# A plain down product for one group in the first token block, its weight sums made a block later

## The chip, the cores and the metric

The kernel runs on one core of one Trainium2 chip. Its engines are TensorE (PE, whose weight loads the profile lists as PEld), VectorE (DVE), ScalarE (ACT), GpSimd (POOL) and SyncE (SP), which issues all of the kernel's DMAs. The metric is the device time of one execution in microseconds, as the median of several runs.

## The reference

The reference is one inference step of a hybrid encoder layer on 2048 prompt tokens and 32 sample tokens, in 32-bit floats: a mixer, then a feed-forward, then a last norm. The part that this case touches is the feed-forward:

```python
h = rmsnorm(x, norm_ffn_g[l]) * (1 + sc2) + sh2
x = x + gt2 * (jnp.square(jax.nn.relu(h @ w_up[l])) @ w_down[l])
...
y = rmsnorm(x, final_norm_g)
```

Here `x` has 2080 rows of 1024 values, `w_up` is 1024 x 4096 and `w_down` 4096 x 1024.

## The kernel before

All tensors are held transposed: 128 features on the partitions, tokens along the free dimension. Each 32-bit operand of a matmul is split in two parts of lower precision: ACT copies it to the high part, DVE subtracts that from the value and gets the low part (`split`, and `operand` around it). A product is then three matmuls into one PSUM bank: high x high, high x low, low x high (`mm3`, line 400 through `mms`). Nearly every vector instruction goes through a helper, so most rows of the profile have one of five lines: 339 (ACT), 354 (a DVE or POOL operation on two tensors), 359 (DVE, one tensor times a scalar, then plus a third), 392 (a DMA) and 400 (a matmul).

The feed-forward (`feed_forward`) runs over three token blocks b = 0, 1, 2 of 696, 696 and 688 tokens, each in two halves g of 348 or 344 columns. The 4096 hidden features are cut into 16 slices s of 256; two slices make one of eight groups q. For a block, slice after slice is computed by `ffn_up`, and each group is multiplied by its rows of `w_down` by `ffn_down`, in two parts u, which differ in the output features (four of the eight tiles m each). The up products of the next group stand between them: down part 0 of group q, up slice 2q+2, down part 1, up slice 2q+3. Sixteen accumulators in SBUF, one per m and g, take the sum over the groups.

Both products use Strassen's scheme in Winograd's form: of a 2 x 2 arrangement of blocks, seven products are made in place of eight, at the price of sums of the operands before and of the results after. Of the hidden tiles the scheme needs seven operands per tile pair (`hidden` and the first lines of `ffn_up`: B11, B21, B22, and the differences T1 to T4); of the weights it needs seven as well, four of them sums. Of the seven products, several add into the same PSUM bank after it has been read: in a part u the pair B1 takes B11, T2, T1 and B22, and between them DVE (`add`) adds what stands in the bank to an accumulator. That makes 14 additions for each part.

The weight sums are made once. In block 0 (`down_weights`, `b` false) four raw 128 x 512 tiles of `w_d` are loaded, POOL makes four sums or differences, and all seven operands are split; the four pairs made of sums are also stored to DRAM (`sd_d`, two stores each). In blocks 1 and 2 three raw tiles are loaded and split, and the four kept pairs are loaded (`kept`). The up weights are handled alike. The split pairs stand in a ring of nine places (`wr`), the raw tiles in one of eight (`raws`).

Groups 0 to 5 add the bank's content to the accumulator (line 354). Ahead of group 6 (`SETTLE`) `settle` multiplies each accumulator by the gate and adds the residual `x`, which it loads from DRAM (`x_d`); from group 6 on an addition multiplies by the gate itself (line 359). After group 7 come the squares for the last norm, whose sums POOL makes, and `final`, which writes the output. The next block's seven sets of four up operands come about in two steps: `h2_values` (called after slice 8) makes them and writes them to DRAM (`th_d`), `h2_load` (after slice 15) loads them through a ring of six places (`fe`, which `settle` uses too) and splits them into the places of the current block's operands (on DVE for block 1, half on POOL for block 2).

The last group of the last block already has a plain form: `plain(b, q)` is true there, `ffn_up` then prepares only the hidden tiles themselves as operands, and `ffn_last` makes the eight products of the 2 x 2 arrangement.

The order of the instructions is worked out when the program is built (`Program.schedule`). Every operation is recorded with an engine, an estimated duration and what it needs. The planner then walks through an estimated time and lets each engine take the most urgent of the operations that are ready; matmuls of the big products have the place in the program as due time, and what they need inherits it. It also keeps POOL and DVE apart where both read SBUF. So a change of the recorded operations can move everything behind it. On the chip each engine then runs its list strictly in order, SP's DMAs as well.

Of the kernel before, what the change touches and what calls it, by code (L numbers as in the profile page):

```python
# [31 lines left out]
GB = [348, 348, 344]  # L32
FT = [0, 696, 1392]
G = 348
NB = 3
SETTLE = 6
SLABW = 8 * WZ
NC_ = 17
SLOT = 1056
# [17 lines left out]
CHAIN, INV, LOCAL, EVAC, GEMM, IDLE = range(6)  # L57
# [16 lines left out]
class Mem:  # L74
# [7 lines left out]
    def view(self, lo, shape, real):  # L82
        n = int(np.prod(shape[1:]))
        a = self.arr[lo : lo + n].reshape(tuple(shape[1:]) + (self.arr.shape[1],))
        a = np.moveaxis(a, -1, 0)[: shape[0]]
        return View(self, a, a, real, ())
# [238 lines left out]
class Kern:  # L325
# [153 lines left out]
    def slab(self, src, n):  # L479
# [4 lines left out]
        def fn():  # L484
            cell["h"] = self.slabs.tile([P, SLABW], F32R, tag=f"wh{k}", name="wh")
            cell["l"] = self.slabs.tile([P, SLABW], F32R, tag=f"wl{k}", name="wl")

        wh = self.wmem[k][0].view(0, (P, SLABW), lambda: cell["h"])
        wl = self.wmem[k][1].view(0, (P, SLABW), lambda: cell["l"])
        self.p.op(NONE, 0.0, fn, [wh, wl], [])  # L490
# [46 lines left out]
    def setup(self):  # L537
# [10 lines left out]
        self.rcol = [sb(f"rcol{k}", [P, 4]) for k in range(2)]  # L548
        self.raw1 = [sb("wr0", [P, SLABW // 2])]
        self.raws = list(self.raw1)  # L550
        self.wmem = [(Mem(SLABW), Mem(SLABW)) for _ in range(2)]
        self.nslab, self.sn = 0, None
# [937 lines left out]
    def down_weights(self, b, u):  # L1490

        quad = lambda q: self.i["w_d"][u, q]
        get = lambda q: self.raw(self.raws, quad(q))
        sd, wr = self.sd_d[u], self.wr
        if b:
            for q, k in ((0, None), (None, 2), (None, 1), (1, None), (None, 0), (3, None), (None, 3)):
                yield self.kept(wr, sd[k]) if q is None else self.operand(wr, get(q))
            return
        a11, a21, a22, a12 = (get(q) for q in (0, 2, 3, 1))
        s1, s2 = (self.turn(self.raws) for _ in range(2))  # L1500
        self.tt(s1, a21, a22, ALU.add, POOL)
        self.tt(a21, a11, a21, ALU.subtract, POOL)
        self.tt(s2, s1, a11, ALU.subtract, POOL)
        yield self.operand(wr, a11)
        yield self.operand(wr, a21, sd[2])
        yield self.operand(wr, s2, sd[1])
        yield self.operand(wr, a12)
        yield self.operand(wr, s1, sd[0])
        yield self.operand(wr, a22)
        self.tt(a12, a12, s2, ALU.subtract, POOL)  # L1510
        yield self.operand(wr, a12, sd[3])

    def plain(self, b, q):
        return (b, q) == (NB - 1, 7)

    def feed_forward(self):
        sl = self.slot
        cell = {}

        def fn():  # L1520
            for k in range(2):
                cell[k] = [self.slabs.tile([P, SLABW], F32R, tag=f"w{x}{k}", name=f"w{x}") for x in "hl"]

        view = lambda k, e: self.wmem[k][e].view(0, (P, SLABW), lambda: cell[k][e])
        wv = [[view(k, e) for e in range(2)] for k in range(2)]
        self.p.op(NONE, 0.0, fn, [v for w in wv for v in w], [])
        self.wr = [tuple(wv[k][e][:, 512 * j : 512 * j + 512] for e in range(2)) for k in (self.nslab % 2, (self.nslab + 1) % 2) for j in range(4)]
        hid = (9, 10, 11, 2, 17, 18, 19, 20, 24)
        for s in (4, 6, 7, 5) + hid:
            self.era(s, F32R)  # L1530
        third = lambda v: [v[:, G * e : G * e + G] for e in range(3)]
        cut = lambda *ss: [x for s in ss for x in third(sl(s, 0, (P, SLOT)))]
        more = cut(4, 6, 7)
        places = [hl for k in range(KT) for hl in zip(third(self.BH[k]), third(self.BL[k]))]
        places += list(zip(more[:4], more[4:8]))
        self.hp = [places[4 * i : 4 * i + 4] for i in range(7)]
        r = cut(*hid) + more[8:]
        self.rp = list(zip(r[::2], r[1::2]))
        two = lambda s: [sl(s, 512 * e, (P, 512)) for e in range(2)]
        self.wr.append(tuple(two(5)))  # L1540
        self.raws = two(0) + two(1) + two(8) + [self.raw1[0][:, 512 * e : 512 * e + 512] for e in range(2)]
        a = [sl(s, G * e, (P, G)) for s in (12, 13, 14, 15, 16) for e in range(3)] + [sl(*self.spare[0], (P, G))]
        self.acc = [a[2 * m : 2 * m + 2] for m in range(KT)]
        self.fbanks = list(range(8))
        self.h2_load(0)

        def up(b, s, ops):
            self.ffn_up(b, s, self.up_weights(b, s), ops)
            if s == 8 and b < NB - 1:
                self.h2_values(b + 1)  # L1550
            if s == 15 and b < NB - 1:
                self.h2_load(b + 1)

        for b in range(NB):
            ops = {}
            for e in range(2):
                up(b, e, ops)
            for q in range(8):
                if q == SETTLE:
                    self.settle(b)  # L1560
                then = {}
                for u, _ in enumerate(self.ffn_last(b, q, ops) if self.plain(b, q) else self.ffn_down(b, q, ops)):
                    if q < 7:
                        up(b, 2 * q + 2 + u, then)
                ops = then
# [108 lines left out]
    def add(self, b, q, m, g, ps, first=False, last=False):  # L1674

        a = self.acc[m][g]
        if q == 0 and first:
            self.act(a[:, : GB[b]], ps, AF.Copy)
        elif q < SETTLE:
            self.tt(a[:, : GB[b]], ps, a[:, : GB[b]], ALU.add)  # L1680
# [52 lines left out]
    def ffn_last(self, b, q, ops):  # L1733
# [18 lines left out]
                self.final(b, g, self.ssq[g][1:])  # L1752
        yield

    def square(self, b, m, g):

        end = (b, g) == (NB - 1, 1)
        a = self.acc[m][g][:, : GB[b]]
        if self.ssq[g] is None or self.ssq[g][0] != b:
            sa = self.piece("fs", b)  # L1760
            self.ssq[g] = [b, sa]
            self.act(sa, a, AF.Square)
            return
        x = self.piece("fp" if end and m == 7 else "fx", b)
        self.act(x, a, AF.Square)
        sa = self.ssq[g][1]
        if end and m in (6, 7):
            self.ssq[g].append(x)
        else:
            self.tt(sa, sa, x, ALU.add, DVE if end else POOL)  # L1770
# [88 lines left out]
```

## Time and profile before

| | |
|---|---|
| Median of 3 runs | 2353.92 us (2351.38 to 2355.38) |
| The profiled execution's own time | 2350.23 us |
| Its span, from the first to the last instruction | 2348.5 us |
| Mean granted TensorE clock in the span | 0.994 |

In the profile an engine's busy time is the time in which at least one of its instructions ran. Matmuls overlap: one of 348 columns lasts some 0.32 us, but the next starts after about half of that. A row of instructions names output and inputs by the program's buffers, numbers left out: `f` is a PSUM bank of the feed-forward, `s` a tile in one of the general SBUF slots (accumulators, hidden tiles, raw weights and some split ones), `wh` and `wl` split weights, `BH` and `BL` split up operands, `wr` another place for raw weights, `modc` the gates, `w_u` and `w_d` the weights in DRAM. Behind the bar of a row stand busy us, the mean ns of one, and the idle time just before with what ended it. A row of waits gives who waited for whom, then us in total, how often, and the longest. Times within the span are counted from its start.

### The profile page before, as it was taken

The page shows a single profiled execution, that of the slowest core. Times are in us where ns is not written, and L with a number is a line of the kernel's source. Part 1 is how long each engine was busy: PE and PEld are TensorE (multiplying, and loading weights), DVE is VectorE, ACT ScalarE, POOL GpSimd, SP SyncE. Part 2 cuts the span into 40 slices and gives each one's busy share as a digit, 9 for nine tenths or more (in the row PEclk, how much of TensorE's full clock was granted, in tenths as well). Part 3 has the DMA queues.
Part 4 walks back from the last instruction along what each step waited for, and adds up shares of the span by engine and source line. Part 5 has one row for each costly group of instructions (what it writes and reads, how often), then busy time and mean ns, then how long its engine had stood idle before and what let it go on. Part 6 is the DMA issues. An engine that isn't in the chain of part 4 may idle for free. (4 is left out here: it accounts for less than half of the span.)

```text
span 2348.5 us, 45724 instructions
## 1 busy us (share of the span) xinstructions
PE 2299.2 (98%) x15882; PEld 2171.3 (92%) x15882; DVE 1678.7 (71%) x3675; ACT 1226.9 (52%) x2817; POOL 598.8 (25%) x827
## 2 busy tenths in 40 slices
PE   7999999999999999999999999999999999999998
PEld 4877878999999888999999989999999999999998
DVE  6556557666665656589999999877667786666775
ACT  4465657455565535376555646664433564334343
POOL 2235421312432322445444434210000050000001
PEclk9999999999999999999999999999999999999999
DMA  9698668465557778888777787998667797666771
GB/s 321 225 333 280 199 189 258 141 187 178 151 175 228 241 220 251 256 269 270 243 252 259 258 269 248 335 323 266 211 219 250 251 294 247 214 220 219 238 232 53
DMA packets 369263, 556.27 MB, mean 237 GB/s; under 512 B 71212, under 2 KB 191424, under 8 KB 369032
## 3 DMA queue, kind: packets, MB, share of 16 engines
q1 hardware_dynamic: 369032, 553.35, 72.8%
q8 instruction: 125, 2.05, 0.4%
q14 instruction: 106, 0.87, 0.1%
HBM read 398.92 MB, written 154.28 MB: 236 GB/s over the span
## 5 line engine op out<-in xcount | busy, mean ns | idle before, releaser
L339 ACT ACTIVATE s<-s 128x348 fp32r<-128x348 f32 (+13 forms) x1079 | 494.9, 482 | 365.3 <-DVE s L354 145.5
L400 PE MATMUL f<-s,wh 128*128 128x348 f32 (+1 forms) x2760 | 662.0, 322 | 6.7 <-DVE s L359 5.4
L400 PEld LDWEIGHTS f<-s,wh 128*128 128x128 f32 x2760 | 480.2, 189 | 10.2 <-DVE s L359 6.2
L354 DVE TENSOR_TENSOR s<-f,s 128x348 f32<-128x348 f32 (+1 forms) x696 | 348.9, 514 | 175.3 <-PE f L400 174.2
L400 PE MATMUL f<-s,wl 128*128 128x348 f32 (+1 forms) x1380 | 444.1, 322 | 0.3 <-DVE wl L354 0.3
L400 PE MATMUL g<-BH,wh 128*128 128x512 f32 (+2 forms) x1112 | 421.8, 379 | 0.7 <-DVE s L359 0.7
L400 PE MATMUL g<-BH,wl 128*128 128x512 f32 (+2 forms) x1112 | 391.7, 352 | 0.0
L354 DVE TENSOR_TENSOR s<-s,s 128x348 fp32r<-128x348 f32 (+9 forms) x688 | 356.4, 547 | 49.2 <-ACT s L339 21.2
L400 PE MATMUL g<-BL,wh 128*128 128x512 f32 (+2 forms) x1112 | 390.6, 351 | 0.0
L400 PE MATMUL f<-BL,wh 128*128 128x348 f32 (+1 forms) x1016 | 329.0, 324 | 4.9 <-DVE BL L354 4.9
L400 PE MATMUL f<-BH,wl 128*128 128x348 f32 (+1 forms) x1016 | 328.1, 323 | 1.1 <-DVE wl L354 1.1
L400 PE MATMUL f<-BH,wh 128*128 128x348 f32 (+1 forms) x1016 | 328.4, 323 | 0.0
L339 ACT ACTIVATE wh<-s 128x512 fp32r<-128x512 f32 (+1 forms) x278 | 174.4, 634 | 240.1 <-PE f L400 180.9
L354 POOL TENSOR_TENSOR s<-s 64x39 f32<-64x39 f32 (+12 forms) x299 | 156.3, 523 | 433.9 <-issue 380.8
L400 PEld LDWEIGHTS f<-s,wl 128*128 128x128 f32 x1380 | 260.2, 189 | 0.6 <-DVE wl L354 0.6
L354 POOL TENSOR_TENSOR s<-s,s 128x512 f32<-128x512 f32 (+5 forms) x154 | 190.9, 1249 | 270.7 <-ACT s L339 118.4
L354 DVE TENSOR_TENSOR wl<-s,wh 128x512 fp32r<-128x512 f32 (+1 forms) x278 | 221.1, 803 | 20.4 <-ACT wh L339 20.0
L400 PEld LDWEIGHTS g<-BH,wh 128*128 128x128 f32 x1112 | 210.3, 189 | 23.8 <-issue 7.4
L400 PEld LDWEIGHTS g<-BH,wl 128*128 128x128 f32 x1112 | 209.2, 188 | 19.2
L400 PEld LDWEIGHTS g<-BL,wh 128*128 128x128 f32 x1112 | 210.6, 189 | 14.4 <-DVE BL L354 0.2
L359 DVE SCALAR_TENSOR_TENSOR s<-s,s,s 128x256 f32<-128x256 f32 (+5 forms) x318 | 161.9, 526 | 63.9 <-ACT s L339 39.6
L400 PEld LDWEIGHTS f<-BL,wh 128*128 128x128 f32 x1016 | 192.3, 189 | 6.5 <-DVE BL L354 6.5
(115 smaller groups left out, 3363.2 us busy)
## 6 DMA issues: line engine op xcount, KB each, us to landing
s<-w_u SPq DMA_DIRECT2D x124, 256.0 KB, 3.8
s<-w_d SPq DMA_DIRECT2D x118, 256.0 KB, 3.1
wh<-su_d SPq DMA_DIRECT2D x113, 256.0 KB, 3.6
wl<-su_d SPq DMA_DIRECT2D x113, 256.0 KB, 3.9
wh<-sd_d SPq DMA_DIRECT2D x108, 256.0 KB, 3.1
wl<-sd_d SPq DMA_DIRECT2D x108, 256.0 KB, 3.7
wr<-w_b SPq DMA_DIRECT2D x42, 512.0 KB, 5.0
s<-adaw SPq DMA_DIRECT2D x32, 512.0 KB, 5.9
```

The costliest lines, as they stand in the source:

```text
L339: self.p.op(ACT, c, lambda: nc.scalar.activation(out=R(out), in_=R(in_), func=func, **{k: R(v) for k, v in kw.items()}), [out, accum], [in ...
L354: self.p.op(eng, c, lambda: e.tensor_tensor(out=R(out), in0=R(a), in1=R(b), op=op), [out], [a, b])
L359: self.p.op(DVE, c, lambda: nc.vector.scalar_tensor_tensor(out=R(out), in0=R(a), scalar=R(s), in1=R(b), op0=op0, op1=op1), [out], [a, s, b])
L400: nc.tensor.matmul(R(out), R(l), R(r), **kw)
```

## The change

Group 6 of block 0 is added to the cases with a plain down product. `plain` is true for it, so slice 13 puts only the eight hidden tiles of the group (2 x 2 halves, two tiles each) into operand form and makes no differences. A new function `ffn_plain` loads and splits the four raw weight tiles of a part and, for each half g and each of the four output tiles, runs twelve matmuls into a bank of its own and adds it to the accumulator once. The weight sums of that group can then not be taken from block 0: in `down_weights` the branch that makes and stores them now also holds for block 1 in this group (`b > (u // 2 in PLAIN)`); block 2 loads them as before.

```diff
+PLAIN = (6,)
...
-        if b:
+        if b > (u // 2 in PLAIN):
             for q, k in ((0, None), (None, 2), (None, 1), (1, None), (None, 0), (3, None), (None, 3)):
                 yield self.kept(wr, sd[k]) if q is None else self.operand(wr, get(q))
             return
...
     def plain(self, b, q):
-        return (b, q) == (NB - 1, 7)
+        return (b, q) == (NB - 1, 7) or b == 0 and q in PLAIN
...
-                for u, _ in enumerate(self.ffn_last(b, q, ops) if self.plain(b, q) else self.ffn_down(b, q, ops)):
+                for u, _ in enumerate((self.ffn_down if not self.plain(b, q) else self.ffn_last if b else self.ffn_plain)(b, q, ops)):
...
+    def ffn_plain(self, b, q, ops):
+
+        for u in range(2):
+            w = [self.operand(self.wr, self.raw(self.raws, self.i["w_d"][2 * q + u, x])) for x in range(4)]
+            for g in range(2):
+                for i in range(2):
+                    for j in range(2):
+                        m = 4 * i + 2 * u + j
+                        ps = self.take(GB[b])
+                        for e in range(2):
+                            wh, wl = w[2 * i + e]
+                            for k in range(2):
+                                c = slice(256 * k + 128 * j, 256 * k + 128 * j + 128)
+                                with self.p.at(GEMM):
+                                    self.mm3(ps[1], wh[:, c], wl[:, c], *ops[(e, g)][k], e == k == 0, e == k == 1)
+                        self.add(b, q, m, g, ps[1], first=True, last=True)
+                        self.give(ps)
...
+            yield
```

On every engine the planned order is as before until slice 13 of block 0, and again from some way into group 0 of block 2. The added constant shifts all lines of helpers by one, so line 354 is 355 in the new kernel, 359 is 360, and so on.

The first place is DVE at the start of group 6 of block 0. In the rows `s_481` to `s_485` are accumulators, `s_494` and `s_495` loaded residuals, `s_490` to `s_492` hidden tiles, `s_` names with five digits parts of operands, `f_` a bank. Before:

```order
L359 SCALAR_TENSOR_TENSOR s_481<-f_15459,modc,s_481 128x348
L354 TENSOR_TENSOR s_11772<-s_490,s_11731 128x348
L354 TENSOR_TENSOR s_492<-f_15426,s_491 128x348
L354 TENSOR_TENSOR wl<-s_469,wh 128x512
L359 SCALAR_TENSOR_TENSOR s_481<-s_481,modc,s_494 128x348
L354 TENSOR_TENSOR s_495<-s_494,s_495 128x348
L359 SCALAR_TENSOR_TENSOR s_481<-f_15465,modc,s_481 128x348
L354 TENSOR_TENSOR s_11970<-s_492,s_11970 128x348
L354 TENSOR_TENSOR s_490<-s_490 128x348
L354 TENSOR_TENSOR wl<-wr_96,wh 128x512
```

The same place in the new kernel:

```order
L360 SCALAR_TENSOR_TENSOR s_483<-s_483,modc,s_495 128x348
L360 SCALAR_TENSOR_TENSOR s_481<-f_15461,modc,s_481 128x348
L360 SCALAR_TENSOR_TENSOR s_481<-s_481,modc,s_494 128x348
L360 SCALAR_TENSOR_TENSOR s_481<-f_15481,modc,s_481 128x348
L360 SCALAR_TENSOR_TENSOR s_482<-s_482,modc,s_495 128x348
L360 SCALAR_TENSOR_TENSOR s_482<-s_482,modc,s_494 128x348 x2
L360 SCALAR_TENSOR_TENSOR s_483<-s_483,modc,s_494 128x348
L360 SCALAR_TENSOR_TENSOR s_485<-s_485,modc,s_495 128x348
L360 SCALAR_TENSOR_TENSOR s_483<-f_15487,modc,s_483 128x348
L355 TENSOR_TENSOR wl<-s_470,wh 128x512 x2
```

Before, additions out of PSUM (`f_` as input), residuals, operand splits, differences and weight splits alternate; now the splits and differences are fewer and mostly ahead, and seven residual additions stand in front of or between the first three additions out of PSUM.

The second place is DVE where the first low halves of block 1's up operands are made (`BL`). Before, among the last additions of group 7:

```order
L359 SCALAR_TENSOR_TENSOR s_485<-f_16285,modc,s_485 128x348
L354 TENSOR_TENSOR wl<-s_477,wh 128x512
L354 TENSOR_TENSOR BL_79<-s_494,BH_71 128x348
L359 SCALAR_TENSOR_TENSOR s_482<-f_16366,modc,s_482 128x348
L359 SCALAR_TENSOR_TENSOR s_483<-f_16371,modc,s_483 128x348
```

In the new kernel, among the up products of slice 15, ahead of group 7:

```order
L360 SCALAR_TENSOR_TENSOR s_472<-f_15928,modc,s_472 128x348
L355 TENSOR_TENSOR wl<-s_469,wh 128x512
L355 TENSOR_TENSOR BL_79<-s_494,BH_71 128x348
L355 TENSOR_TENSOR BL_79<-s_495,BH_71 128x348
L355 TENSOR_TENSOR s_10260<-s_477,s_10260 128x512
L355 TENSOR_TENSOR s_491<-f_15973,s_491 128x348
```

The first six of the 28 low halves have moved ahead of all of group 7's additions; the other 22 still stand between and behind the last of them.

The third place is POOL in block 1. Before, the loads for block 2 (`BL`) follow the preparation of block 2's operands directly:

```order
L354 TENSOR_TENSOR s_494<-s_494,s_496 128x344
L354 TENSOR_TENSOR s_495<-s_495,s_496 128x344
L354 TENSOR_TENSOR BL_79<-s_495,BH_71 128x344
L354 TENSOR_TENSOR BL_80<-s_494,BH_72 128x344
L354 TENSOR_TENSOR BL_80<-s_495,BH_72 128x344
```

In the new kernel:

```order
L355 TENSOR_TENSOR s_495<-s_495,s_496 128x344
L355 TENSOR_TENSOR wr_96<-s_470,s_477 128x512
L355 TENSOR_TENSOR s_470<-s_470 128x512
L355 TENSOR_TENSOR wr_96<-wr_96,s_470 128x512
L355 TENSOR_TENSOR s_477<-s_477,wr_96 128x512
L355 TENSOR_TENSOR wr_96<-s_477 128x512
L355 TENSOR_TENSOR s_477<-s_470,s_477 128x512
L355 TENSOR_TENSOR s_469<-wr_96,s_470 128x512
L355 TENSOR_TENSOR wr_96<-wr_96,s_469 128x512
L355 TENSOR_TENSOR BL_79<-s_495,BH_71 128x344
```

The eight weight sums of group 6 (128 x 512) stand here now, between the two; in block 0 they are gone.

More of the change, by code (lines that the diff above doesn't have):

```diff
@@ L1753, in ffn_last @@
         yield
+    def ffn_plain(self, b, q, ops):
[14 more added lines that the diff above has]
+                        self.give(ps)
+            if q == 7 and u == 1:
+                for g in range(2):
+                    self.final(b, g, self.ssq[g][1:])
+            yield
     def square(self, b, m, g):
```

## The prediction

> **What bounds the kernel now.** I read the page's busy shares first, then a table of equal stretches of 25 us, then PE's own waits, then single rows where PE falls short.
>
> ```profile
> PE 2299.2 (98%) x15882; PEld 2171.3 (92%) x15882; DVE 1678.7 (71%) x3675; ACT 1226.9 (52%) x2817; POOL 598.8 (25%) x827
> ```
>
> PE is busy 98% of the span: the kernel is bound by PE wherever PE isn't made to wait, and a matmul added there costs its whole time. The shares hide that the first token block of the feed-forward is unlike the others. The stretches show it (columns: stretch, length, then busy us and instructions of PE, PEld, DVE, ACT, POOL, then granted clock, DMA share, GB/s):
>
> ```profile
> 1050.00:1375.00 325.00, 322.74 (x2007) 319.56 (x2006) 317.20 (x538) 195.94 (x391) 153.70 (x103) 1.00 0.75 256
> 1350.00:1375.00 25.00, 25.00 (x159) 25.00 (x158) 24.86 (x43) 14.19 (x28) 11.35 (x8) 1.00 0.91 302
> 1375.00:1400.00 25.00, 19.61 (x107) 18.75 (x106) 24.13 (x46) 11.10 (x24) 5.83 (x4) 0.86 0.79 246
> 1400.00:1425.00 25.00, 25.00 (x159) 25.00 (x158) 24.28 (x41) 12.13 (x24) 12.12 (x8) 1.00 0.82 283
> 1425.00:1450.00 25.00, 24.61 (x153) 24.05 (x151) 23.52 (x46) 18.67 (x40) 8.21 (x6) 1.00 0.52 181
> 1450.00:1475.00 25.00, 21.80 (x129) 20.52 (x129) 25.00 (x43) 13.03 (x28) 17.01 (x15) 0.99 0.88 300
> 1475.00:1500.00 25.00, 24.91 (x143) 24.87 (x144) 21.63 (x39) 19.86 (x46) 12.72 (x12) 0.88 0.98 320
> 1550.00:1850.00 300.00, 300.00 (x1882) 300.00 (x1881) 211.88 (x433) 128.84 (x264) 3.66 (x4) 1.00 0.77 246
> 1850.00:1875.00 25.00, 25.00 (x159) 25.00 (x158) 19.71 (x37) 12.19 (x27) 3.95 (x4) 1.00 0.77 248
> 1900.00:1925.00 25.00, 24.33 (x158) 23.75 (x158) 19.62 (x34) 16.97 (x39) 16.18 (x16) 1.00 0.88 298
> ```
>
> In the long stretch of the second block PE is full: one matmul costs 300 / 1882 = 0.159 us, and a full 25 us show 159. Counts measure lost time better than busy time, because they also show matmuls at a low clock. In the first block DVE is busy nearly without a gap; in the second it has room (212 of 300 us) and POOL rests. From 1375 to 1500, which holds groups 6 and 7 of the first block and the change to the second, PE misses 52 + 0 + 6 + 30 + 16 = 104 matmuls, 104 x 0.159 = 16.5 us. PE's waits in that time, and two fine stretches, say why:
>
> ```profile
> PE f L400 <- DVE s L359: 5.4, 2, 3.2
> PE f L400 <- DVE BL L354: 2.3, 3, 1.6
> PE f L400 <- DVE s L354: 1.1, 1, 1.1
> ```
> ```profile
> 1388.00:1392.00 4.00, 1.79 (x8) 1.51 (x9) 4.00 (x8) 0.00 (x0) 1.00 (x1) 0.64 0.88 264
> 1392.00:1396.00 4.00, 4.00 (x16) 4.00 (x15) 4.00 (x8) 1.26 (x2) 0.26 (x1) 0.51 0.79 247
> ```
>
> All are waits for DVE. The 5.4 us are for L359, the scaled additions out of PSUM in group 6: a bank can take no further product until DVE has read it. Behind them the granted clock is 0.51 for 4 us: PE is busy throughout, with 16 matmuls in place of 25. So 5.4 us of waiting cost 52 matmuls, 8.3 us. BL are the low halves of the next block's operands.
>
> **The change part by part.** PE: the seven products of one half take 84 matmuls, the plain one 96; two halves make 24 more, 24 x 0.159 = +3.8 us, which nothing hides on a full PE.
>
> DVE, first block. The price is the distance between starts, a little under a duration:
>
> ```profile
> 1374.32 3.96 DVE L354 TENSOR_TENSOR s<-s,s 128x348 f32<-128x348 f32 x9
> 1389.67 0.57 DVE L359 SCALAR_TENSOR_TENSOR s<-s,modc,s 128x348 f32<-128x348 f32 x1
> 1390.17 0.68 DVE L354 TENSOR_TENSOR s<-wr,s 128x512 fp32r<-128x512 f32 x1
> 1390.77 0.57 DVE L359 SCALAR_TENSOR_TENSOR s<-f,modc,s 128x348 f32<-128x348 f32 x1
> ```
>
> (3.96 - 0.51) / 8 = 0.43 us for 348 columns, 0.50 for a scaled addition, 0.60 for a weight split. Gone are 8 differences of hidden tiles (3.4), 6 of 14 operand splits (2.6), 6 of 14 weight splits (3.6) and 12 of 28 additions (6.0): 15.6 us. The eight sums also leave POOL, and a working POOL slows DVE. The same shapes on DVE, first from 1040 to 1475, where POOL ran 140 instructions, then from 1550 to 1850, where it ran 4:
>
> ```profile
> L354 DVE TENSOR_TENSOR wl<-s,wh 128x512 fp32r<-128x512 f32 x136 | 118.9, 887 | 5.7 <-ACT wh L339 5.3
> L354 DVE TENSOR_TENSOR s<-f,s 128x348 f32<-128x348 f32 x229 | 111.5, 511 | 3.9 <-PE f L400 3.6
> L354 DVE TENSOR_TENSOR s<-s,s 128x348 f32<-128x348 f32 x70 | 47.5, 686 | 0.1
> ```
> ```profile
> L354 DVE TENSOR_TENSOR s<-f,s 128x348 f32<-128x348 f32 x197 | 100.2, 518 | 69.2 <-PE f L400 69.0
> L354 DVE TENSOR_TENSOR wl<-s,wh 128x512 fp32r<-128x512 f32 x44 | 30.3, 689 | 4.8 <-ACT wh L339 4.8
> L354 DVE TENSOR_TENSOR s<-s,s 128x348 f32<-128x348 f32 x38 | 19.2, 515 | 2.1 <-ACT s L339 2.1
> ```
> ```profile
> 1040.00:1475.00 435.00, 423.77 (x2612) 417.88 (x2610) 423.98 (x724) 259.90 (x522) 202.83 (x140) 0.99 0.75 256
> ```
>
> An addition that reads PSUM isn't slowed (511 against 518 ns); one that reads SBUF twice is, by 198 and 171 ns. Over these two groups that is 136 x 0.198 + 70 x 0.171 = 39 us, or 0.28 us for each of 140 POOL instructions: eight fewer give 2.2 us. The ends are 0 and a full stop of DVE for each sum's 202.83 / 140 = 1.45 us, 11.6 us; I take the row's mean. DVE is relieved of about 18 us between 1362 and 1467, more than the 16.5 us that PE misses, so PE itself is late next and not DVE.
>
> By that relief alone all 16.5 would come back. I leave some, by the nearest rows. Groups 0 to 5 of the same block have the same tight DVE: in 325 us 325 / 0.159 = 2039 matmuls would fit, 2007 ran, 32 x 0.159 = 5.1 us over some six groups, 0.85 each. So groups 6 and 7 keep 1.7 of 58 x 0.159 = 9.2 us: -7.5. The plain form's own wait, for the last operands of slice 13 at its start, lies in that 1.7; its bounds are 0 and 3. The change of blocks misses 46 matmuls, 7.3 us; two norm products stand there too, so not all of it is waiting. The next change of blocks, in the stretch from 1900, with half of the splits on POOL, misses 1. The splits come earlier now:
>
> ```profile
> 1462.33 0.51 DVE L354 TENSOR_TENSOR BL<-s,BH 128x348 fp32r<-128x348 f32 x1
> 1462.87 0.32 SPq L392 DMA_DIRECT2D s<-th_d  x1
> 1465.80 0.94 DVE L354 TENSOR_TENSOR BL<-s,BH 128x348 fp32r<-128x348 f32 x2
> 1466.34 0.80 SPq L392 DMA_DIRECT2D s<-th_d  x2
> 1467.50 0.32 PE L400 MATMUL f<-BH,s 128*128 128x348 f32 x1
> ```
>
> Before, the first of 28 splits runs at 1462, five microseconds ahead of the second block's first matmul at 1467.5, since the order puts it among group 7's last additions; each split frees one of six landing places, and the next load is issued at once. In the new order six splits stand inside slice 15; behind it come group 7's 168 matmuls, so they have 27 to 40 us of PE time ahead of their use. Between 0 and 7.3 I take 3.0 as left: -4.3.
>
> DMA and SP, first block: the same eight weight loads, 16 stores of 256 KB fewer. Nothing waits for those stores, so 0; that SP and ACT (12 splits' high halves fewer) are freer is worth nothing on its own.
>
> Second block: eight sums on POOL, and 8 more weight splits, 8 x 0.60 = 4.8 us on DVE plus 2.2 us of slowing; ACT gets 8 more high halves. 16 loads of kept sums go, 2 raw loads and 16 stores come. DVE's idle share there is 88 of 300 us, some 16 in a group of 53 us, and POOL is empty; the sums stand ahead of the loads for the next change of blocks. Cost 0. If that cover were gone it would be up to 7 us, of which PE could see what exceeds the slack.
>
> The Trainium skill, "SBUF — State Buffer", section "Who interferes with whom", states that a DVE instruction with two SBUF inputs contends with a GpSimd instruction that reads SBUF and that the second to issue fully blocks. The trace agrees in kind (887 against 689 ns, and 511 against 518 for PSUM). Taken at full length for every sum, the rule would give DVE 27 us of relief in the first block and 16.4 us of load in the second.
>
> The sum: +3.8 - 7.5 - 4.3 + 0 = -8.0 us. The profiled execution took 2350.2 us, 3.7 below the median of the runs, 2353.9 (2351.4 to 2355.4); against it the new time is 2342.2, against the median 2345.9.
>
> **The rivals.**
>
> *The change of blocks doesn't get better.* What PE waits for there may be the chain of six landing places, not DVE's total: a load takes about 4 us, and POOL's square sums still run beside the splits. For it: the load follows the split by 0.03 us each time. Against it: six splits now run ahead. Then -7.5 + 3.8 = -3.7: 2350.2.
>
> *Slower: the waits stay, and PE pays.* In the new order seven of the additions that bring in the residual (they need loads of x2) stand in front of or between the first additions of group 6. If one of these loads is late, DVE, which runs in order, stands with everything behind it: the operands of slice 14, the additions, the splits. For it: these loads share the six places with the next block's operands, and POOL waited for one:
>
> ```profile
> POOL wr L354 <- DMA s<-x_d: 4.4, 1, 4.4
> s<-x_d SPq DMA_DIRECT2D x64, 174.0 KB, 4.0
> ```
>
> Against it: DVE has no wait for such a load in 1360 to 1500. If DVE's relief is eaten so, 16.5 stays missing and +3.8 is paid: 2357.7; one landing of 4.0 us more makes 2361.7. The sign turns where less than 3.8 of the 16.5 comes back.
>
> *The moved sums stop DVE in the second block.* If each stops DVE for its whole 1.45 us, DVE gets 8 x 1.45 + 4.8 = 16.4 us in a group with some 16 to spare; a run of them just ahead of their use would let PE wait, I estimate 2 to 3 us: 2348.4. The full-stop rule of the skill's page, above, leads there. Against it: the rows' mean of 0.28 us.
>
> **How the numbers follow.** A run of this kernel tells 0.2%, 4.7 us, from no change. The forecast has a chance of 0.64, nearly all of it faster (0.62, same 0.02). The unchanged change of blocks: 0.18 (faster 0.06, same 0.12). The waits that stay: 0.12 (same 0.03, slower 0.09). The stopped DVE: 0.06 (faster 0.04, same 0.02). Together faster 0.72, same 0.19, slower 0.09. The low end is all waits gone, 2353.9 - 16.5 + 3.8 = 2341.2, less 1.2 for the spread of runs: 2340. The high end takes in the second case with its spread and reaches a gain of nothing: 2354. The forecast alone spans 2341 to 2349.
>
> **What would show it.** Right: some 155 or more matmuls in every stretch between 1375 and 1425; no wait for L360 (the same addition, one line further down) above 1 us; no clock near 0.5 in group 6; the first BL split more than 20 us ahead of the second block's first matmul; that matmul some 5 us earlier than at 1467.5; PE full through the second block with POOL now busy there. Wrong: PE still waiting for the scaled additions or for BL at the old lengths, DVE rows that wait for x2 loads, or counts under 157 from 1780 to 1860.

## The result, and the profile after

The changed kernel takes 2343.39 us (median of 6 runs, 2340.94 to 2347.76), the kernel before 2353.36 us beside it (6 runs, 2348.38 to 2355.38). The ratio is 0.9964, with a 95% interval of 0.9953 to 0.9975: 0.36% or some 8 to 10 us faster, where 8.0 was forecast. The span of the profiled execution is 2341.5 us, 7.0 less than before.

The page's busy shares of the changed kernel:

```profile
PE 2300.4 (98%) x15906; PEld 2171.5 (93%) x15906; DVE 1664.8 (71%) x3651; ACT 1227.0 (52%) x2813; POOL 598.0 (26%) x827
```

PE has 24 instructions more and is busy 1.2 us longer: what it gains does not show in its busy time, since PE was also "busy" with matmuls at half the clock before. DVE has 24 instructions and 13.9 us less. The stretches of the changed kernel (columns as above: busy us and instructions of PE, PEld, DVE, ACT, POOL, then clock, DMA share, GB/s):

```profile
1375.00:1400.00 25.00, 24.89 (x156) 24.43 (x155) 21.15 (x38) 10.40 (x21) 5.39 (x4) 1.00 0.87 297
1400.00:1425.00 25.00, 25.00 (x159) 25.00 (x158) 18.99 (x34) 12.38 (x26) 5.88 (x4) 1.00 0.56 188
1425.00:1450.00 25.00, 25.00 (x158) 25.00 (x158) 25.00 (x48) 19.01 (x42) 7.68 (x6) 1.00 0.60 204
1450.00:1475.00 25.00, 24.63 (x157) 24.34 (x156) 24.18 (x45) 14.88 (x33) 14.88 (x14) 1.00 0.98 334
1475.00:1500.00 25.00, 25.00 (x161) 24.71 (x160) 24.61 (x46) 22.18 (x52) 11.87 (x11) 1.00 1.03 371
1500.00:1525.00 25.00, 25.00 (x156) 24.61 (x155) 14.96 (x29) 14.01 (x31) 1.83 (x2) 1.00 0.95 319
1525.00:1550.00 25.00, 24.72 (x154) 24.14 (x153) 19.34 (x42) 15.74 (x34) 1.85 (x2) 1.00 0.96 311
1550.00:1575.00 25.00, 24.46 (x152) 23.94 (x151) 17.54 (x35) 11.63 (x24) 2.00 (x3) 1.00 0.95 313
1780.00:1860.00 80.00, 80.00 (x503) 80.00 (x503) 65.16 (x124) 37.89 (x77) 13.09 (x11) 1.00 0.79 253
```

From 1375 to 1500 PE runs 791 matmuls where 691 ran before, and the clock is 1.00 throughout. PE's waits in that time are down to a single one, and it is for the last norm, not for the products:

```profile
PE M L401 <- POOL s L355: 0.4, 1, 0.4
```

What the first of these tables also shows is a loss that was not there before: from 1500 to 1575 PE runs 462 matmuls, 14 to 15 fewer than the 477 of full stretches (before: 159 + 159 + 158).

To compare kernels whose stages lie at different times, I take each stage by itself from here on: the time from its first matmul to the first of the next stage, less the number of its matmuls of the two big products times 0.1594 us. The result is what PE lost in it; the small matmuls of the last norm are not counted and so stand in it:

| us lost by PE | before | after |
|---|---|---|
| block 0, slice 13 to slice 15 (group 6) | 8.25 | 0.51 |
| block 0, group 7 | 2.19 | 0.03 |
| change of blocks (slices 0 and 1 and the first part of group 0 of block 1; some 2.3 of it are matmuls of the last norm) | 8.12 | 2.86 |
| block 1, the rest of groups 0 and 1 | 0.1 | 2.5 |

This gives -7.7 - 2.2 - 5.3 + 2.4 = -12.8, and +3.8 for the 24 matmuls makes -9.0. Elsewhere the feed-forward began 1.0 us later in this execution, block 2 lost 1.3 more, and the first block outside these stages 0.6 less. That comes to -7.3, beside a span that is 7.0 shorter.

### The profile page after: what moved, and what is told of

It reads as the page before. It is cut to its first block, busy times and chain, and to the rows that moved or that the text cites. A ratio compares the mean times of both kernels' runs of the same rounds, so it can differ in the third digit from the quotient of the medians.

```text
span 2341.5 us, 45700 instructions
## 1 busy us (share of the span) xinstructions
PE 2300.4 (98%) x15906; PEld 2171.5 (93%) x15906; DVE 1664.8 (71%) x3651; ACT 1227.0 (52%) x2813; POOL 598.0 (26%) x827
## 4 chain that ended last, share of the span: by engine, by line
PE 77%; DVE 8%; DMA 6%; ACT 3%; issue 2%; POOL 2%; SPq 1%; POOLq 0%; DVEq 0%; ACTq 0%
PE f L401 43%; PE g L401 26%; DVE s L355 5%; PE C L401 3%; ACT s L340 2%; PE B L401 2%; DVE wl L355 2%; POOL s L355 1%; DMA s<-th_d 1%; PE L L401 1%; DVE s L360 1%; PE M L401 1%; PE L L412 1%; SPq L393 1%; DVE BL L355 1%
## 5 line engine op out<-in xcount | busy, mean ns | idle before, releaser
L355 DVE TENSOR_TENSOR s<-s,s 128x348 fp32r<-128x348 f32 (+9 forms) x679 | 351.7, 546 | 54.6 <-ACT s L340 19.9
```

The source lines that it names most:

```text
L355: self.p.op(eng, c, lambda: e.tensor_tensor(out=R(out), in0=R(a), in1=R(b), op=op), [out], [a, b])
```

## The experiments

Each kernel was timed in turn with the kernel before on the same chip, and its ratio is to that kernel, which took 2352.28 us in the first set (light load, old load, sums kept, late values), 2350.57 in the second (fewer additions, sums again, late values in the kernel before, plain elsewhere) and 2350.86 in the third. Two ratios can be told apart from some 3 to 4 us on.

**What made the waits go: the load of DVE or the form of the product?** Two kernels part what the plain product joins. The first keeps the Strassen products with their banks that are handed over, and gives DVE the light load.

```diff
+        if self.light(b, q):
+            for name, key in (("B11", (0, 0)), ("T1", (0, 1)), ("B21", (1, 0)), ("T4", (1, 0)), ("T2", (1, 1)), ("T3", (1, 1)), ("B22", (1, 1))):
+                ops[name] = ops[key]
...
         def add(ps, ms, g, first=False, last=False):
+            if self.light(b, q) and ps is not B1:
+                return
```

> The seven products of the Strassen form (84 matmuls a half) stay in group 6 of block 0, with the banks handed over as before three times in each part; but DVE gets the plain form's work only: 8 operand splits, 8 weight splits, 16 additions, no differences, the sums made in block 1. Operands and 12 additions are left out, so group 6 of block 0 computes something else; only its time is meant. Theory A, DVE's load is what PE waited for: all waits go as in the changed kernel and 24 matmuls are not paid: 2343.4 - 3.8 = 2339.6, between 2338 and 2341.5. Theory B, what helped is that a bank takes one product only and need not be handed over: the 8.2 us of waits in group 6 stay, 2339.6 + 8.2 = 2347.8 or more.

Measured: 2339.24 us, ratio 0.9938 (0.9926 to 0.9951). Its losses are 1.9 in group 6, 0.0 in group 7, 3.0 in the change of blocks. So with a light DVE the hand-overs cost little: 1.9 us in group 6, where the changed kernel loses 0.5. The 24 matmuls not paid are seen in the time, though not by themselves. The kernel is 4.2 us under the changed kernel by the medians and 6.1 by the ratios, with 2.2 to 10.0 by their intervals; by the stages it is 3.8 for the matmuls and 0.9 for smaller losses (5.0 in place of 5.9 in the four rows of the table). Theory A holds here.

The second keeps the plain product and gives DVE the old load.

```diff
+        hi, lo = ops.setdefault(name, {})[m] = self.operand(self.rp, x)
+        if isinstance(name, tuple) and self.block == 0:
+            for _ in range(1 if name == (1, 1) else 2):
+                self.tt(lo, x, hi.f32(), ALU.subtract)
...
+                if x < 3:
+                    self.tt(w[x][1], r, w[x][0].f32(), ALU.subtract)
...
+                        if (i, j) != (1, 1):
+                            t = self.acc[m][g][:, : GB[b]]
+                            self.stt(t, ps[1], 0.0, t, ALU.mult, ALU.add)
```

> The changed kernel, with DVE's work of the Strassen form given back in group 6 of block 0 as repeated splits and additions of zero (14 operand-sized splits, 6 weight splits, 12 additions out of PSUM, 15.6 us); PE's 96 matmuls a half, the banks used once, and the sums on POOL in block 1 stay. Theory A: most of the 13.8 us that came back is lost again: 2343.4 + 13.8 = 2357, or 2.2 less, since POOL's sums don't return: 2354 to 2358. Theory B: the load of DVE doesn't matter, 2343.4, at most 2346.

Measured: 2346.63 us, ratio 0.9975 (0.9966 to 0.9984). By the ratios that is 2.6 us later than the changed kernel, with the intervals from 0.7 earlier to 5.9 later, where theory A expected 11 to 14. Stretches and PE's waits from 1375 to 1500 of this kernel:

```profile
1375.00:1400.00 25.00, 24.49 (x152) 23.88 (x151) 23.60 (x47) 10.00 (x19) 4.51 (x3) 1.00 0.82 271
1400.00:1425.00 25.00, 25.00 (x158) 25.00 (x158) 24.54 (x44) 12.31 (x27) 7.38 (x5) 1.00 0.68 217
1450.00:1475.00 25.00, 23.21 (x139) 21.50 (x138) 22.12 (x43) 13.29 (x28) 14.50 (x14) 1.00 0.95 322
```
```profile
PE f L401 <- ACT BH L340: 0.9, 1, 0.9
PE f L401 <- DVE s L355: 0.4, 1, 0.4
PE f L401 <- DVE BL L355: 0.3, 1, 0.3
```

DVE is as busy as before the change (23.6 and 24.5 of 25 us), but PE loses only 1.7 us in group 6 and 0.4 in group 7. The change of blocks loses 6.7, nearer to the 8.1 before than to 2.9. So theory A fits the change of blocks and is only half the truth for group 6: there PE waits where a full DVE and banks that must be read before the next product may go on come together. Taking away either is enough: 8.3 with both, 1.9 with the hand-overs alone, 1.7 with the load alone, 0.5 with neither. Rows of DVE in this kernel show that a late DVE matters less here:

```profile
1384.54 0.57 DVE L360 SCALAR_TENSOR_TENSOR s<-f,modc,s 128x348 f32<-128x348 f32 x1
...
1390.00 0.58 DVE L360 SCALAR_TENSOR_TENSOR s<-f,modc,s 128x348 f32<-128x348 f32 x1
```

These are the first two additions that take in a product of group 6; the third came at 1394.8. PE was through with the first part of the group, eight banks, at 1391.9, so six of the eight were read after that, and yet PE lost only 0.4 us in the up slice that followed. Not all of the fall from 8.3 to 1.7 has to come from the banks, though. The plain product also gives PE 3.8 us more to do in the group, time in which a late DVE catches up, and of the old load POOL's sums did not return in this kernel (2.2 us by the prediction's estimate). These shares were not parted.

The change of blocks goes with the place of the BL splits. In the changed kernel and in the one with the light load, six or more of them run some 30 us or more ahead of the second block's first matmul. With the old load the first one runs at 1457.7, 4 us ahead of that matmul at 1461.6, much as before the change (1462.3 and 1467.5). The planner sets that place, so the load of DVE and the new order that comes with it are not parted either.

A smaller dose of relief, in the kernel before:

```diff
         def add(ps, ms, g, first=False, last=False):
+            if (b, q) == (0, 6) and ps is not B1:
+                return
```

> The kernel before, with 12 of the 28 additions of group 6 of block 0 left out (those of the two banks pairs that are not handed over three times), so that its result there is another; 6.0 us of DVE's work less, all splits, differences, sums and three of four hand-overs as before. If PE waits in group 6 because DVE is behind by a queue of work: the 8.2 us of waits there shrink by up to 6.0, and the change of blocks keeps most of its loss: 2352.3 - 6 = 2346, between 2344 and 2348. If the hand-overs alone make the wait: 2352 less 1, 2350.5 or more.

Measured: 2347.35 us, ratio 0.9987 (0.9978 to 0.9996), 3 us. Group 6 loses 5.6 in place of 8.3, group 7 0.4 in place of 2.2, the change of blocks 8.3 and the groups after it 0.9. The longest waits of this kernel in group 6 are not for the additions any more, but for what DVE had to make behind them:

```profile
PE f L400 <- DVE wl L354: 2.2, 1, 2.2
PE f L400 <- DVE s L354: 1.9, 2, 1.6
```

So DVE's queue is what PE meets, as theory A says, but 6.0 us less work gave back 4.5 us there, and 1 was lost again behind it.

**What the moved sums bought.** The plain product, with the sums left in block 0:

```diff
-        if b > (u // 2 in PLAIN):
+        if b:
...
+            for x, k in ((a21, 2), (s2, 1), (s1, 0), (a12, 3)):
+                self.operand(self.wr, x, sd[k])
```

> Plain product in group 6 of block 0, but its weight sums are still made, split and stored there (block 1 loads them as before): DVE has 8 more weight splits than in the changed kernel, 4.8 us, and POOL the eight sums, 2.2 us by their slowing. DVE's relief is then 11 us against 16.5 us that PE missed. Theory A: 16.5 - 11 = 5.5 us of waiting left: 2343.4 + 4 to 5.5, 2347 to 2349. Rival, only the product's form counts and the moved sums bought nothing: 2343.4, within 1.

Measured: 2347.48 us, ratio 0.9977 (0.9968 to 0.9987), 3.1 us later than the changed kernel by the ratios. Group 6 loses 1.6, group 7 0.5, the change of blocks 6.2 and the rest of groups 0 and 1 of block 1 1.1. The 3.1 us are at the edge of what two ratios can tell; the losses by stage, 9.4 in place of 5.9, agree with them. Most of the price is in the change of blocks: with the sums, the first BL split runs at 1457.2 again, 4 us ahead of the second block's first matmul at 1461.2. So the plain product freed most of group 6 even with the sums there, and the change of blocks was freed only where DVE had neither the sums' splits nor the old load.

And what the same sums cost in block 1, where block 0 makes them as well and only no longer stores them (16 stores fewer):

```diff
+        if not b and u // 2 in PLAIN:
+            sd = (None,) * 4
...
-        return (b, q) == (NB - 1, 7) or b == 0 and q in PLAIN
+        return (b, q) == (NB - 1, 7)
```

> The kernel before; the weight sums of group 6 are made in block 0 for its own use and not stored, and made again, split and stored in block 1: the second block gets exactly what the change moves there, and the first block loses 16 stores. The prediction's term for the second block, 0: 2352.3, within 1.5. Rival, each sum stops DVE for its whole length: +2 to +3, 2355.

Measured: 2348.62 us, ratio 0.9996 (0.9987 to 1.0005), so between 3.1 us less and 1.2 more. PE is full where the sums are made (second row: the kernel before):

```profile
1780.00:1860.00 80.00, 80.00 (x503) 80.00 (x502) 64.22 (x125) 35.61 (x71) 10.89 (x8) 1.00 0.77 253
```
```profile
1780.00:1860.00 80.00, 80.00 (x504) 80.00 (x503) 58.27 (x117) 30.50 (x61) 0.00 (x0) 1.00 0.80 252
```

**What the plain product costs where nothing waits.** The same form in group 4 of block 1:

```diff
-        return (b, q) == (NB - 1, 7) or b == 0 and q in PLAIN
+        return (b, q) == (NB - 1, 7) or (b, q) == (1, 4)
```

> The kernel before, with the plain product in group 4 of block 1 in place of group 6 of block 0, all sums in block 0 as before. DVE has room there and PE no waits, so the 24 matmuls should cost their whole time and nothing comes back: 2352.3 + 3.8 = 2356.1, between 2355 and 2357. Rival, the plain form is nearly free wherever it stands (fewer hand-overs, fewer splits): 2352.3 to 2353.5.

Measured: 2356.04 us, ratio 1.0022 (1.0013 to 1.0031), 5.2 us with 3.1 to 7.3. The stretches of this kernel, cut at the first matmuls of the two plain parts and of the up slices behind them, give the price more sharply:

```profile
1719.74:1735.07 15.33, 15.33 (x99) 15.33 (x98) 6.46 (x13) 3.39 (x6) 0.00 (x0) 1.00 0.29 98
1735.07:1748.49 13.42, 13.42 (x86) 13.42 (x85) 5.76 (x11) 6.30 (x12) 0.00 (x0) 1.00 0.61 190
```

A plain part, of 96 matmuls, takes 15.33 us, and the up slice behind it, of 84 matmuls like a part in Strassen's form, 13.42: 1.91 more, twice, 3.8 us. The same form only costs time where DVE has room.

**The new loss in block 1.** The step that makes the operand values for block 2 (`h2_values`) issues its first load at 1492.4 in the changed kernel and at 1512.6 before, 20 us earlier, where the down product of group 0 begins 11 us earlier; and the DMA system is full there. Held back by a dependence on the last matmul that the program recorded ahead of it:

```diff
+        late = (max(i for i, o in enumerate(self.p.ops) if o.eng == PE),) if b == 2 else ()
         for g in range(2):
-            self.dma(r[g], self.r2_d[:, self.span(b, g)])
+            self.dma(r[g], self.r2_d[:, self.span(b, g)], after=late)
...
-                    self.dma(x, self.x2_d[kk][:, self.span(b, g)])
+                    self.dma(x, self.x2_d[kk][:, self.span(b, g)], after=late)
```

> The changed kernel, with the loads for block 2's up operands (the step that makes their values) held back until the matmuls of slice 8 of block 1 have been planned, in place of groups 0 and 1 of block 1. Theory C, the 2.5 us that PE newly loses in groups 0 and 1 of block 1 come from these transfers sharing a full DMA system with the weights: 2343.4 - 2.5 = 2341, the DMA share from 1500 to 1575 below 0.9. Rival, the loss there is of another cause (the second block simply meets late weights): 2343.4 within 1, or later if the values come too late for block 2.

Measured: 2339.07 us, ratio 0.9945 (0.9933 to 0.9958). The loss in groups 0 and 1 of block 1 is 0.1 now, and the stretches of this kernel are full:

```profile
1500.00:1525.00 25.00, 25.00 (x159) 25.00 (x158) 12.44 (x25) 12.57 (x27) 0.00 (x0) 1.00 0.83 276
1550.00:1575.00 25.00, 25.00 (x158) 25.00 (x158) 14.27 (x29) 9.08 (x18) 0.00 (x0) 1.00 0.67 219
```

It has the lowest time of all the kernels that compute the whole reference, though the kernel with POOL's values, further down, can't be told apart from it. The same edit in the kernel before is the control:

> The kernel before, with the loads of block 2's operand values held back as in the run of late values. If the 2.5 us in groups 0 and 1 of block 1 arise only since the changed kernel comes there 11 us earlier into a full DMA system: no loss stood there before, so nothing to win: 2352.3, within 1.2. Rival, late loads help every version: -3 to -4.5, 2348 to 2349.

Measured: 2350.64 us, ratio 1.0001 (0.9992 to 1.0011). So the loss belongs to the changed kernel. That a full DMA system was its cause does not follow yet: the kernel with the light DVE load has a DMA share as high in this time (1.01, 0.95 and 0.93 from 1500 to 1575) and loses 0.1 there. The rows of the changed kernel's DVE show another way (behind the bar of a row, in brackets: idle time just before it, and what ended it):

```profile
1515.98 0.52 DVE L355 TENSOR_TENSOR s<-s,s 128x344 f32<-128x344 f32 x1 [2.04 <-DMA s<-r_d]
...
1534.90 0.56 DVE L355 TENSOR_TENSOR s<-s,s 128x344 f32<-128x344 f32 x1 [2.07 <-DMA s<-x_d]
...
1542.33 0.52 DVE L355 TENSOR_TENSOR s<-s,s 128x344 f32<-128x344 f32 x1 [1.52 <-DMA th_d<-s]
...
1544.23 4.39 DVE L355 TENSOR_TENSOR s<-s,s 128x348 f32<-128x348 f32 x10
```

The rows of 344 columns are block 2's values. DVE stands in front of them for a load or a store, and work for the running block, behind them in the list, starts late and then in one rush of ten. To tell the two apart, POOL gets DVE's part of the values, and the transfers stay:

```diff
-                    self.tt(x, x, r[g], ALU.mult, POOL if g else DVE)
+                    self.tt(x, x, r[g], ALU.mult, POOL if g or b > 1 else DVE)
...
+            eng = POOL if b > 1 else DVE
...
-            self.tt(t1, b12, b11, ALU.subtract)
+            self.tt(t1, b12, b11, ALU.subtract, eng)
...
```

> The changed kernel, with DVE's part of making block 2's operand values (8 products and 16 differences) given to POOL; the transfers and their time stay where they are. If PE's new 2.5 us in groups 0 and 1 of block 1 come from DVE standing, in its order, in front of work on these values that waits for a transfer, they go: 2343 - 2.5 = 2340.5, with the DMA share between 1500 and 1575 still above 0.9. If it is the full DMA system itself that brings the weights late: no gain, 2343 within 1.

Measured: 2340.05 us, ratio 0.9951 (0.9938 to 0.9964), 3.1 us less than the changed kernel by the ratios, at the edge of what they can tell. The stretches show it more sharply:

```profile
1525.00:1550.00 25.00, 25.00 (x158) 25.00 (x157) 16.58 (x34) 16.23 (x34) 10.33 (x12) 1.00 0.98 325
1550.00:1575.00 25.00, 25.00 (x159) 25.00 (x158) 17.11 (x29) 12.41 (x26) 11.55 (x12) 1.00 0.93 315
```

The DMA share is 0.98 and 0.93, near the changed kernel's 0.96 and 0.95, and PE loses 0.1 in groups 0 and 1. DVE's waits for these loads and stores (`x_d`, `r_d`, `th_d`), 9.7 us from 1500 to 1580 in the changed kernel, are gone; POOL has them now. So it was DVE standing in its order, and not the full DMA system by itself. Why these operations met late transfers in the changed kernel and not before, by their new order or by the new time, was not parted.

**Why group 6.** Two more kernels, both from the kernel before, move the 16 residual additions of `settle`.

```diff
-SETTLE = 6
+SETTLE = 5
```

> The kernel before, with the 16 residual additions made ahead of group 5 and not 6, in all blocks. If group 6 of block 0 stalls because they (16 x 0.50 = 8 us) come on top of a DVE that is full: the 8.2 us of loss leave group 6 and stand in group 5; the time stays, 2351 within 2. If the stall belongs to group 6 for another reason (the values for block 1, made there too): 8 us stay there.

Measured: 2353.38 us, ratio 1.0007 (0.9998 to 1.0015). The stall is in group 5 now (10.3 us), with 2.4 left in group 6 and 0.0 in group 7. The residual additions bring it with them.

```diff
-                if q == SETTLE:
-                    self.settle(b)
+                self.settle(b, [m for m in range(KT) if q == self.turns(b, m)])
...
+    def turns(self, b, m):
+        return SETTLE if b else 3 + m % 4
```

> The kernel before, with block 0's 16 residual additions spread over groups 3, 4, 5 and 6, four ahead of each; the Strassen form everywhere. If they are what tips DVE over in group 6: the stall there shrinks from 8.2 to under 3, without the 3.8 for the plain form, while each later addition of the early settled tiles costs 0.07 us more (some 84 of them, 6 us of DVE): 2351 - 5 = 2346, between 2343 and 2348. If DVE's total in block 0 decides, nothing is won: 2350 or more, the 6 us even make it later.

Measured: 2365.01 us, ratio 1.0055 (1.0042 to 1.0067): 13 us slower, where 5 faster was expected. PE's waits from 1266 to 1345 of this kernel, and DVE's:

```profile
PE f L400 <- DVE s L359: 7.1, 2, 6.8
PE f L400 <- DVE s L354: 3.2, 4, 1.9
PE f L400 <- DVE wl L354: 1.4, 2, 1.0
```
```profile
DVE wl L354 <- ACT wh L339: 5.3, 4, 2.2
DVE s L359 <- DMA s<-x_d: 2.6, 2, 2.3
DVE s L354 <- DMA s<-x_d: 2.2, 1, 2.2
```

There is one great stall in groups 4 and 5 (some 24 us) in place of the one in group 6, and in it DVE stands for loads of x2 and for ACT. Spreading the additions did not take them off DVE. How much of the 24 us is the 6 us of extra work on later additions, and how much the loads, was not parted.

## Why the prediction was right

The time came out at 2343.4 us for 2345.9, inside the range, and faster as forecast. The terms, one by one:

- *PE, +3.8.* Right: 3.8 us by the stage in block 1, where the same form was tried by itself. The kernel that keeps 84 matmuls agrees, less sharply.
- *Groups 6 and 7, -7.5.* The waits are gone as it says: no wait for line 360 at all, the clock at 1.00. By stages the gain is 9.9. Two things were mis-sized: the loss before was 10.4 and not 9.2 (the second half of group 7 lies in the stretch from 1450, which I had given to the change of blocks), and what is left is 0.5 and not 1.7.
- *The reason for it*, "DVE is relieved of about 18 us", was incomplete. The relief is enough, as the light load shows, but in group 6 most of it was not needed: with the old load on DVE the plain product still waits for little. The step overlooked that the plain product takes another bank for each output tile and hands none over, so that a late DVE no longer stops PE at once, and that PE's 3.8 us more are time for DVE too.
- *The change of blocks, -4.3.* Right in its mechanism, measured -5.3: here the load, or the order of BL splits that comes with it, decides, since 6.7 us stay with the old load and 6.2 with the sums left in block 0. The first BL split starts at 1424.3, 37 us ahead of the second block's first matmul, which comes at 1461.8, 5.7 us earlier than before.
- *Second block, 0.* Right for the moved sums (-0.9 us, at most +1.2), wrong for the block. The step that failed is "the sums stand ahead of the loads for the next change of blocks. Cost 0": it looked at what the sums add to block 1, and not at what else moves forward there. Block 2's operand values came earlier too, DVE stood in front of their transfers, and PE lost 2.4 us more in groups 0 and 1. This cancelled most of the underestimate of 3.4 us in the two terms above. That the sum came out nearer than its terms is luck.

Of the rivals, *the change of blocks doesn't get better* is refuted for the changed kernel and is what happens when the sums stay in block 0. *Slower: the waits stay* did not come about, but its mechanism exists. DVE did wait for loads of x2 in the time it named (2.7 us in three waits, the longest 1.1), and PE did not feel it there:

```profile
DVE s L360 <- DMA s<-x_d: 2.7, 3, 1.1
```

The same mechanism took 2.4 us in block 1, and far more where the residual additions were spread. *The moved sums stop DVE* is refuted. The same two groups of DVE from 1780 to 1860, before, and in the changed kernel, where POOL ran 11 instructions, eight of them the moved sums:

```profile
L354 DVE TENSOR_TENSOR wl<-s,wh 128x512 fp32r<-128x512 f32 x10 | 6.9, 689 | 2.4 <-ACT wh L339 2.4
...
L354 DVE TENSOR_TENSOR wl<-wr,wh 128x512 fp32r<-128x512 f32 x5 | 3.4, 688 | 2.4 <-ACT wh L339 2.4
```
```profile
L355 DVE TENSOR_TENSOR wl<-s,wh 128x512 fp32r<-128x512 f32 x18 | 12.4, 695 | 3.3 <-ACT wh L340 3.3
...
L355 DVE TENSOR_TENSOR wl<-wr,wh 128x512 fp32r<-128x512 f32 x6 | 4.7, 788 | 2.4 <-ACT wh L340 2.4
```

They grew by 18 x 6 ns and 6 x 100 ns, together 0.7 us for 11 POOL instructions. The prediction's rate of 0.28 us each would have given 3.1, a full stop for as long as POOL was busy 13.1. This holds for these orders, in which the planner keeps POOL and DVE apart where it can.

What stays open: the light kernel and the loaded kernel also differ in the planner's order, so the sizes 1.9 and 1.7 are of these two orders, and only the fall from 8.3 is safe. How much of it the hand-overs alone would make, with PE's work the same, was not tried.

## What to carry to other kernels

A wait of a full PE for a full vector engine has two handles, the work in front and the moment at which the result must have been read; try them one at a time, since only one may be worth its price. Here 24 more matmuls paid in the group where both came together, and the same form in a group without waits cost its whole 3.8 us; other groups were not tried. When a stage gets faster, look at what starts earlier behind it: work for a later block, placed ahead in an in-order engine, can wait for a transfer with urgent work behind it, and giving it to an idle engine or holding its loads back won some 3 to 4.5 us more.

## What the runs showed of the hardware that was not expected

The granted clock falls without any long wait. In the kernel that settles ahead of group 5, the longest wait of PE between 1326 and 1346 is 1.4 us:

```profile
PE f L400 <- DVE s L359: 2.4, 2, 1.4
```
```profile
1330.00:1334.00 4.00, 2.83 (x17) 2.28 (x15) 4.00 (x10) 1.92 (x5) 0.00 (x0) 1.00 0.57 183
1334.00:1338.00 4.00, 1.50 (x6) 0.96 (x6) 4.00 (x5) 1.89 (x4) 2.86 (x2) 0.87 0.76 247
1338.00:1342.00 4.00, 2.83 (x9) 2.38 (x9) 4.00 (x9) 0.64 (x2) 0.66 (x1) 0.50 0.79 251
1342.00:1346.00 4.00, 4.00 (x14) 4.00 (x15) 4.00 (x9) 1.09 (x2) 0.94 (x1) 0.50 0.67 238
```

After 4 us in which PE was busy for 1.5, the clock is 0.50 for 8 us, and in the last 4 of them PE is busy throughout and runs 14 matmuls in place of 25. In the kernel with fewer additions, waits of up to 2.2 us left the clock at 1.00:

```profile
1388.00:1392.00 4.00, 2.02 (x13) 1.73 (x11) 4.00 (x7) 1.27 (x2) 1.47 (x1) 1.00 0.83 234
1392.00:1396.00 4.00, 3.77 (x23) 3.77 (x24) 3.84 (x7) 1.61 (x3) 1.58 (x1) 1.00 0.89 267
```

So several short waits close together can cost more than one longer one. The longest wait does not settle it here, and the busy share of 4 us doesn't either. In the kernel before, where the second block begins, the longest wait was 1.6 us and PE was busy for 1.96 of 4 us, nearly the 2.02 above, and yet the clock fell behind it:

```profile
1470.00:1474.00 4.00, 1.96 (x11) 1.38 (x10) 4.00 (x8) 3.23 (x8) 2.42 (x3) 1.00 0.92 298
1474.00:1478.00 4.00, 3.75 (x17) 3.33 (x16) 3.48 (x5) 1.76 (x4) 1.83 (x2) 0.55 0.97 301
```

The Trainium skill, "TensorE: Matmul & The Clock Gate", section "HAM oscillation — how this bites in real kernels", gives as the rule no idle gaps of PE above some 3.4 us. These rows don't bear that out as a condition on a single gap; they would fit an activity window of such a length, which the same page of the Trainium skill describes under "What's actually happening". Where such a window begins, no run here shows.
